# Moving SBUF-by-SBUF products from POOL to DVE in the first part of a mixing stage, with the rotary tables scaled later and a key's high part written twice by ACT

## The chip, the cores and the metric

The kernel runs on one core of one Trainium2 chip. The metric is device time in microseconds (us) of one execution. Five engines work side by side, each on its own queue in order: PE (matrix products), DVE (VectorE), ACT (ScalarE), POOL (GpSimd) and SP, which here only issues DMAs. They wait for each other by semaphores.

## The reference

Two encoder layers over a sequence of 512 tokens of width 1024, all in float32. Each layer does

    x += 0.5 * swiglu_1(rms_norm(x))
    z  = rms_norm(x) @ W_in                 # columns for four mixers of four heads each
    A: 2-D neighbourhood attention with a learned bias      (nq, nk, nv)
    B: sliding window attention, rotary, sink logit          (sq, sk, sv)
    C: three dilated windows merged, rotary                  (dq, dk, dv)
    D: latent attention with a decoupled rotary key          (cq, ckv, kpe)
    x += concat(rms_norm of each mixer's output) @ W_out
    x += 0.5 * swiglu_2(rms_norm(x))
    x += sigmoid(rms_norm(x) @ W_gate) * (p @ W_proj)

and a last rms_norm follows. `rope` turns the halves of a vector: (x1 cos - x2 sin, x2 cos + x1 sin). In mixer A a bias is added to each score and everything outside a window is masked.

## The kernel before

Activations lie transposed: 128 partitions of the width, 512 tokens along the row. Every float32 operand of a large product is split in two, a high part rounded to the matrix unit's format and a low part that is the rest, and a product is three matmuls (high by high, high by low, low by high; `mm3y`, L200, one step of three matmuls at a time). Weights are split as they arrive: `pieces` (L155) loads 512 KB into `raw`, ACT writes the high part `wh` (L178), and L179 and L180 subtract it to give the low part `wl`. This subtraction is on POOL while `self.mixing` is true and on DVE otherwise. `raw` has two buffers, `wh` and `wl` three each.

The mixing stage (`mix`, L680) runs once per layer. First it projects nq0 and nk0; behind them the norm's factor `rb` is spread over the partitions (L715) and multiplied in by DVE (`plain`, L358). Then 16 heads run in order, four of each mixer, as a software pipeline: scores of head n (`qk`), transposed probabilities (`tr`) and their product with the values (`pv`) of the head before, and between them steps of the projections still to come (`pump`, with `STEPS` per head). The heads of mixer A are n = 0 to 3.

Tiles that the change touches:

- A key is kept as `t`, whose two halves hold its high part twice, and `klz`, which holds the low part of one head's 64 rows and zeros elsewhere (`stack`, L338, with `scale` None). ACT writes the high part (L344), DVE copies it to the other 64 partitions (L345) and subtracts (L349). It runs for nk0, nk1, sk, dk0 and dk1.
- `rope` (L326): ACT swaps the halves into `sw`, DVE multiplies the projection by `cos`, POOL multiplies `sw` by `sin` (L334), DVE adds.
- L719 and L720 multiply the two rotary tables `cos` and `sin` (names `tab`) by `rb` on POOL, before the first head.
- For each head of mixer A a bias of 128x896 is loaded into `nb` by a DMA from POOL's queue (L649) and subtracted from the mask by POOL (L651). `nb` has one buffer, so the load of a head waits until DVE has read the bias of the head before (L410).
- The scores go to one of four PSUM buffers `s`. L410 adds the mask on DVE, takes the row minimum and so frees the buffer.
- `value` (L363): DVE multiplies a projected value by `rb` (L367), PE transposes it some steps later (L374).

PE's and SP's instructions are issued as the code is written. On DVE, ACT and POOL a scheduler sets the order when the program is built; on the chip each engine keeps that order.

Of the kernel before, what the change touches and what calls it, by code (L numbers as in the profile page):

```python
# [9 lines left out]
F32 = mybir.dt.float32  # L10
F32R = mybir.dt.float32r
AF = mybir.ActivationFunctionType
ALU = mybir.AluOpType
# [21 lines left out]
class Encoder:  # L35
# [119 lines left out]
    def pieces(self):  # L155
        nc, a = self.nc, self.a
        first = True
        for src, cuts in self.plan():
            n = cuts[-1][0] + cuts[-1][1] * cuts[-1][2]
            raw = self.tile("raw", [128, 1024], F32, 2)  # L160
            src = src.rearrange("p k m -> p (k m)") if len(src.shape) == 3 else src
            if first:
                nc.sync.dma_start(raw[:, :512], src[:, :512])
                nc.sync.dma_start(self.x[0], a["x"][:, 0])
                nc.sync.dma_start(self.x[1], a["x"][:, 1])
                nc.sync.dma_start(self.x[2], a["x"][:, 2])
                nc.sync.dma_start(raw[:, 512:], src[:, 512:])
                for k in range(3, KC):
                    nc.sync.dma_start(self.x[k], a["x"][:, k])
                first = False  # L170
            else:
                nc.sync.dma_start(raw[:, :n], src)
            for o, k, m in cuts:
                c = k * m
                hi = self.tile("wh", [128, 512], F32R, 3)[:, :c]
                lo = self.tile("wl", [128, 512], F32R, 3)[:, :c]
                r = raw[:, o:o + c]
                nc.scalar.activation(hi, r, AF.Copy)  # L178
                eng = nc.gpsimd if self.mixing else nc.vector  # L179
                eng.tensor_tensor(out=lo, in0=r, in1=hi.bitcast(F32), op=ALU.subtract)  # L180
                yield (hi.rearrange("p (k m) -> p k m", k=k), lo.rearrange("p (k m) -> p k m", k=k))

    def take(self):
        if not self.ready:
# [141 lines left out]
    def rope(self, p, scale=None):  # L326
        nc = self.nc
        sw = self.tmp()
        for b in range(4):
            o = b ^ 1  # L330
            nc.scalar.activation(sw[32 * b:32 * b + 32], p[32 * o:32 * o + 32], AF.Copy)  # L331
        u = self.tmp()
        nc.vector.tensor_tensor(u, p, self.cosr, op=ALU.mult)
        nc.gpsimd.tensor_tensor(out=sw, in0=sw, in1=self.sinr, op=ALU.mult)  # L334
        nc.vector.tensor_tensor(out=u, in0=u, in1=sw, op=ALU.add)
        return self.stack(u, scale)

    def stack(self, u, scale):  # L338
        nc = self.nc
        t = self.big()  # L340
        lo, up = slice(0, 64), slice(64, 128)
        if scale is None:
            for e, r, w in ((0, lo, up), (1, up, lo)):
                nc.scalar.activation(t[r, e], u[r], AF.Copy)  # L344
                nc.vector.tensor_copy(t[w, e], t[r, e].bitcast(F32))  # L345
            kl = self.klz[self.nkl % 2]
            self.nkl += 1
            for e, r in ((0, lo), (1, up)):
                nc.vector.tensor_tensor(out=kl[r, e], in0=u[r], in1=t[r, e].bitcast(F32), op=ALU.subtract)  # L349
            return t, kl  # L350
        for e, r in ((0, lo), (1, up)):
            nc.scalar.activation(t[r, e], u[r], AF.Copy, scale=scale)
        for e, r, w in ((0, lo, up), (1, up, lo)):
            nc.vector.scalar_tensor_tensor(out=t[w, e], in0=u[r], scalar=scale, in1=t[r, e].bitcast(F32),
                                           op0=ALU.mult, op1=ALU.subtract)
        return t
# [154 lines left out]
        self.t[key] = self.plain(self.p, scale)  # L511

    def d_rope(self, key, i, scale=None):
        yield from self.proj(i)
        self.t[key] = self.rope(self.p, scale)

# [123 lines left out]
    def heads(self, l):  # L640
        nc, a = self.nc, self.a
        S = lambda e: slice(64 * e, 64 * e + 64)
        off, wid = (0, 256, 256, 640), (256, 384, 384, 256)
        base = dict(band=True, sink=None, perm=False)

        def na(h):
            j, e = divmod(h, 2)
            nb = self.tile("nb", [128, 896], F32, 1)
            self.tc.keep_in_program_order(nc.gpsimd.dma_start(nb, a["na_bias"][l, h]))  # L649
            v = nb.rearrange("p (b r w) -> p b r w", b=7, r=8)  # L650
            nc.gpsimd.tensor_tensor(out=v, in0=self.na_mask.unsqueeze(2).to_broadcast([128, 7, 8, 16]),  # L651
                                    in1=v, op=ALU.subtract)
            return dict(base, q=self.t[f"nq{j}"], k=self.t[f"nk{j}"], v=self.t[f"nv{j}"], rows=S(e), odd=e,
                        perm=True, mask=lambda t: nb[:, off[t]:off[t] + wid[t]])

        def swa(i):
            j, e = divmod(i, 2)
            h = 2 * e + j
            return dict(base, q=self.t[f"sq{j}"], k=self.t["sk"], v=self.t["sv"], rows=S(e), odd=e,
                        mask=lambda t: self.swa_mask[:, (128 if t == 0 else 0):(256 if t == 3 else 384)],  # L660
                        sink=(self.nsink[:, l, h:h + 1], self.sink[:, l, h:h + 1]))

        def dil(h):
            j, e = divmod(h, 2)
            return dict(base, q=self.t[f"dq{j}"], k=self.t[f"dk{j}"], v=self.t[f"dv{j}"], rows=S(e), odd=e,
                        band=False, mask=lambda t: self.dil_mask[:, 384 - 128 * t:896 - 128 * t])

        def mla(h):
            j, e = divmod(h, 2)
            return dict(base, q=self.t[f"mq{h}"], k=self.t[f"mk{h}"], v=self.t[f"mv{j}"], rows=None,  # L670
                        odd=e, band=False, mask=None)

        out = []
        for f, gi, keys in ((na, 0, ("nq{0}", "nk{0}", "nv{0}")), (swa, 1, ("sk", "sq{0}", "sv")),
                            (mla, 2, ("mv{0}",)), (dil, 3, ("dv{0}",))):
            for h in range(4):
                out.append((f, gi, h, [k.format(h // 2) for k in keys]))
        return out

    def mix(self, l, nxt):  # L680
        nc, a = self.nc, self.a
# [6 lines left out]
        cos = self.tile("tab", [128, T], F32, 2)  # L688
        sin = self.tile("tab", [128, T], F32, 2)
# [26 lines left out]
        self.t["nq0"] = self.plain(p0, s)  # L716
        self.t["nk0"] = self.plain(p1)
        self.done |= {"nq0", "nk0"}
        nc.gpsimd.tensor_tensor(out=cos, in0=cos, in1=self.rb, op=ALU.mult)  # L719
        nc.gpsimd.tensor_tensor(out=sin, in0=sin, in1=self.rb, op=ALU.mult)  # L720

        self.mixing = True
        last, prev, pend, rg = None, None, None, None
        todo = self.heads(l)
        self.need(*todo[0][3])
# [2 lines left out]
        for n, item in enumerate(todo + [None]):  # L728
            h = None
            if item is not None:  # L730
                f, gi, i, keys = item
                self.need(*keys)
                h = f(i)
                if h["odd"]:
                    h["y"], h["l8"] = mate["y"], mate["l8"]
                else:
                    h["y"], h["l8"] = self.ytile(), self.tile("l8", [128, 2, 4], F32, 2)
                    mate = h
                h["end"] = gi if i == 3 else None
            if n == 9:  # L740
                self.stream += [(f"part{i}", self.d_part(i)) for i in range(4)]
            for b in range(6):
                if b == 0 and last is not None:
                    self.pv(last, 3)
                    if last["odd"]:
                        self.pair_end(last)
                        pend = last["end"]
                if h is not None and b < 4:
                    self.qk(h, b)
                if prev is not None:  # L750
                    if 3 <= b:
                        self.pv(prev, b - 3)
                    if 1 <= b < 5:
                        self.tr(prev, b - 1)
                quota += STEPS[n] / 6.0
                self.pump(int(quota))
                quota -= int(quota)
                if b == 3 and pend is not None:
                    rg = self.rstat(self.gacc, 256)
                if b == 5 and rg is not None:  # L760
                    self.group_end(l, pend, rg)
                    pend, rg = None, None
            last, prev = prev, h
# [24 lines left out]
        for m in range(4):  # L788
            if m % 2 == 0:
                w = self.take()  # L790
# [195 lines left out]
```

## Time and profile before

| | us |
|---|---|
| median of 3 timed runs | 2148.17 (2146.65 to 2148.85) |
| the profiled execution | 2144.82 |
| its span in the trace | 2143.0 |

The profiled execution is 3.35 us below the median of the timed runs, and 1.82 us of it lie outside the span.

| engine | busy us | share of the span |
|---|---|---|
| PE | 2091.5 | 98% |
| DVE | 1210.1 | 56% |
| ACT | 929.2 | 43% |
| POOL | 283.3 | 13% |

PE is busy nearly all the time; what it does not do is found by asking for its waits and then by looking at those places in the order of time. A busy share over the whole span says little about the mixing stages, which are two stretches of about 260 us each, from about 380 us and from about 1437 us.

### The profile page before, as it was taken

How to read it: one execution, taken by the hardware profiler on the slowest of the kernel's cores; microseconds unless marked ns; L12 is line 12 of the kernel's file. 1: busy time of each engine (PE TensorE's matmuls, PEld its weight loads, DVE VectorE, ACT ScalarE, POOL GpSimd, SP SyncE). 2: the span in 40 equal slices, each digit the busy share in tenths (PEclk: the TensorE clock that was granted, in tenths of full speed). 3: DMA queues.
4: the chain of work that ended last, by engine and by line, in shares of the span. 5: the costliest groups of instructions: out<-in, count | busy, mean ns of one | idle time of the engine just before them, and what ended most of it. 6: DMA issues, size and time to landing. Idle time of an engine off the chain costs nothing.

```text
span 2143.0 us, 25740 instructions
## 1 busy us (share of the span) xinstructions
PE 2091.5 (98%) x9564; PEld 1726.3 (81%) x9564; DVE 1210.1 (56%) x1926; ACT 929.2 (43%) x1690; POOL 283.3 (13%) x234
## 2 busy tenths in 40 slices
PE   8999999899999999999999999998999999999997
PEld 6888888777788888888888888886878888888886
DVE  5444445567776444455654444556787744444554
ACT  4332333477754322333433233335777533233343
POOL 2000001444321000001100000025432200000011
PEclk9999999999999999999999999999999999999998
DMA  3233223213112223232322232232221222232322
GB/s 130 98 109 101 98 86 111 95 58 84 40 60 99 99 87 101 97 105 92 100 98 99 93 104 94 89 113 94 64 60 50 69 99 98 85 106 95 107 90 89
DMA packets 63357, 195.37 MB, mean 91 GB/s; under 512 B 7552, under 2 KB 15872, under 8 KB 63232
## 3 DMA queue, kind: packets, MB, share of 16 engines
q1 hardware_dynamic: 61808, 187.92, 26.5%
q0 software_dynamic: 1280, 5.77, 1.0%
q8 instruction: 75, 1.23, 0.2%
q14 instruction: 50, 0.41, 0.1%
q10 hardware_dynamic: 144, 0.05, 0.0%
HBM read 189.51 MB, written 2.10 MB: 89 GB/s over the span
## 4 chain that ended last, share of the span: by engine, by line
PE 91%; DVE 5%; ACT 2%; issue 1%; DMA 1%; POOL 0%; SPq 0%; POOLq 0%; DVEq 0%; ACTq 0%
PE ps L205 15%; PE ps L206 15%; PE ps L207 15%; PE s L207 13%; PE s L205 13%; PE s L206 13%; PE pv L461 2%; PE s L445 2%; PE s L403 1%; DVE klz L349 1%; PE s L404 1%; ACT tmp L331 1%; PE s L230 1%; DVE PT L449 1%; ACT PT L448 0%
## 5 line engine op out<-in xcount | busy, mean ns | idle before, releaser
L178 ACT ACTIVATE wh<-raw 128x512 fp32r<-128x512 f32 (+1 forms) x712 | 437.7, 615 | 959.4 <-PE ps L206 440.7
L180 DVE TENSOR_TENSOR wl<-raw,wh 128x512 fp32r<-128x512 f32 (+1 forms) x614 | 435.4, 709 | 405.8 <-ACT wh L178 399.4
L205 PE MATMUL ps<-act,wh 128*128 128x512 f32 x616 | 248.5, 403 | 5.9 <-ACT act L127 5.9
L221 POOL TENSOR_TENSOR acc<-acc,tmp 128x512 f32<-128x512 f32 x54 | 72.1, 1336 | 1362.8 <-ACT tmp L220 1362.6
L205 PE MATMUL ps<-big,wh 128*128 128x512 f32 x616 | 246.3, 400 | 0.0
L206 PE MATMUL ps<-act,wh 128*128 128x512 f32 x616 | 244.2, 396 | 1.8 <-DVE act L128 1.7
L207 PE MATMUL ps<-act,wl 128*128 128x512 f32 x616 | 243.1, 395 | 0.0
L207 PE MATMUL ps<-big,wl 128*128 128x512 f32 x616 | 241.0, 391 | 0.0
L206 PE MATMUL ps<-big,wh 128*128 128x512 f32 x616 | 241.0, 391 | 0.0
L205 PE MATMUL s<-big,wh 128*128 128x512 f32 x520 | 202.4, 389 | 0.0
L205 PE MATMUL s<-act,wh 128*128 128x512 f32 x520 | 202.4, 389 | 0.0
L207 PE MATMUL s<-act,wl 128*128 128x512 f32 x520 | 202.3, 389 | 0.0
L206 PE MATMUL s<-act,wh 128*128 128x512 f32 x520 | 202.3, 389 | 0.0
L207 PE MATMUL s<-big,wl 128*128 128x512 f32 x520 | 202.3, 389 | 0.0
L206 PE MATMUL s<-big,wh 128*128 128x512 f32 x520 | 202.3, 389 | 0.0
L180 POOL TENSOR_TENSOR wl<-raw,wh 128x512 fp32r<-128x512 f32 (+1 forms) x98 | 128.0, 1306 | 265.2 <-ACT wh L178 259.5
L205 PEld LDWEIGHTS ps<-act,wh 128*128 128x128 f32 x616 | 117.5, 191 | 27.6 <-ACT act L127 6.0
L206 PEld LDWEIGHTS ps<-act,wh 128*128 128x128 f32 x616 | 117.4, 191 | 27.4 <-DVE act L128 6.0
L207 PEld LDWEIGHTS ps<-act,wl 128*128 128x128 f32 x616 | 117.5, 191 | 24.7
L207 PEld LDWEIGHTS ps<-big,wl 128*128 128x128 f32 x616 | 116.2, 189 | 24.9
L206 PEld LDWEIGHTS ps<-big,wh 128*128 128x128 f32 x616 | 116.5, 189 | 21.6
L205 PEld LDWEIGHTS ps<-big,wh 128*128 128x128 f32 x616 | 116.3, 189 | 21.3
(174 smaller groups left out, 3377.6 us busy)
## 6 DMA issues: line engine op xcount, KB each, us to landing
raw<-in_ffn_gu SPq DMA_DIRECT2D x175, 512.0 KB, 3.5
raw<-in_ffn_d SPq DMA_DIRECT2D x64, 512.0 KB, 3.5
raw<-in_w_in SPq DMA_DIRECT2D x40, 512.0 KB, 3.5
raw<-in_ffn_d SPq DMA_DIRECT2D x64, 192.0 KB, 2.5
raw<-in_w_out SPq DMA_DIRECT2D x16, 512.0 KB, 3.5
raw<-in_ple SPq DMA_DIRECT2D x16, 384.0 KB, 3.1
raw<-in_ple SPq DMA_DIRECT2D x16, 256.0 KB, 2.6
nb<-in_na_bias POOLq DMA_DIRECT2D x8, 448.0 KB, 3.6
```

The source lines that it names most:

```text
L178: nc.scalar.activation(hi, r, AF.Copy)
L180: eng.tensor_tensor(out=lo, in0=r, in1=hi.bitcast(F32), op=ALU.subtract)
L205: nc.tensor.matmul(ps, lhsT=wh[:, k], rhs=x[:, 0], start=start and k == 0, stop=False)
L206: nc.tensor.matmul(ps, lhsT=wh[:, k], rhs=x[:, 1], start=False, stop=False)
L207: nc.tensor.matmul(ps, lhsT=wl[:, k], rhs=x[:, 0], start=False, stop=stop and k == last)
L221: eng.tensor_tensor(out=acc, in0=acc, in1=sq, op=ALU.add)
L230: nc.tensor.matmul(ss[:, t:t + 1], lhsT=acc[:, t * 128:(t + 1) * 128], rhs=self.ones, start=True, stop=True)
L331: nc.scalar.activation(sw[32 * b:32 * b + 32], p[32 * o:32 * o + 32], AF.Copy)
L349: nc.vector.tensor_tensor(out=kl[r, e], in0=u[r], in1=t[r, e].bitcast(F32), op=ALU.subtract)
L403: nc.tensor.matmul(s, lhsT=q[:, e, qs], rhs=k[0][:, e, k0:k1], start=True, stop=False)
L445: nc.tensor.transpose(tp[:, t * 128:(t + 1) * 128], h["P"][t][:, o:o + 128], self.ident)
L461: nc.tensor.matmul(pv[:, c], lhsT=vb, rhs=h["pt"][b][:, i, c], start=b == 0 and i == 0, stop=b == 3 and i == 1, skip_group_check=True)
```

## The change

The part of the weights, tables, masks and rotary products that the first heads need moves from POOL to DVE. `mixing` becomes true when head 3 begins and not before head 0, so that the low parts of the weights taken until then are made by DVE, as is the rotary product of `sk` (the new `side`). The subtraction of the bias from the mask is on DVE for all heads of mixer A. The tables are scaled by DVE when the projection of `sk` is started in the code. In `stack`, ACT writes the high part of a key to both places and DVE copies nothing.

```diff
@@ pieces
                 nc.scalar.activation(hi, r, AF.Copy)
-                eng = nc.gpsimd if self.mixing else nc.vector
+                eng = self.side()
                 eng.tensor_tensor(out=lo, in0=r, in1=hi.bitcast(F32), op=ALU.subtract)
...
+    def side(self):
+        return self.nc.gpsimd if self.mixing else self.nc.vector
@@ rope
         nc.vector.tensor_tensor(u, p, self.cosr, op=ALU.mult)
-        nc.gpsimd.tensor_tensor(out=sw, in0=sw, in1=self.sinr, op=ALU.mult)
+        self.side().tensor_tensor(out=sw, in0=sw, in1=self.sinr, op=ALU.mult)
@@ stack
                 nc.scalar.activation(t[r, e], u[r], AF.Copy)
-                nc.vector.tensor_copy(t[w, e], t[r, e].bitcast(F32))
+                nc.scalar.activation(t[w, e], u[r], AF.Copy)
@@ d_rope
+        if key == "sk":
+            for t in (self.cosr, self.sinr):
+                self.nc.vector.tensor_tensor(out=t, in0=t, in1=self.rb, op=ALU.mult)
@@ heads, na
-            nc.gpsimd.tensor_tensor(out=v, in0=self.na_mask.unsqueeze(2).to_broadcast([128, 7, 8, 16]),
+            nc.vector.tensor_tensor(out=v, in0=self.na_mask.unsqueeze(2).to_broadcast([128, 7, 8, 16]),
@@ mix
-        nc.gpsimd.tensor_tensor(out=cos, in0=cos, in1=self.rb, op=ALU.mult)
-        nc.gpsimd.tensor_tensor(out=sin, in0=sin, in1=self.rb, op=ALU.mult)
-
-        self.mixing = True
...
+            if n == 3:
+                self.mixing = True
```

In the new file the lines from `take` to `d_rope` have numbers higher by 3, and those from `d_lat` to the head loop by 6. The order of PE's rows is the same in both programs. In each layer, 12 subtractions for `wl`, 4 for `nb`, 2 for `tab` and 1 rotary product go from POOL to DVE, and 10 copies from DVE to ACT.

The first place is on DVE, at the beginning of the first mixing stage, from the first use of `rb` to the value product of nv0 (L367 before, L370 now). Before:

```order
L360 TENSOR_TENSOR tmp_2905<-ps_2820,rb_2903 128x8x4x16
L360 TENSOR_TENSOR tmp_2912<-ps_2855,rb_2903 128x8x4x16
L354 SCALAR_TENSOR_TENSOR big_2907<-tmp_2905,big_2907 64x512 x2
L345 CAST big_2914<-big_2914 64x512
L349 TENSOR_TENSOR klz_1043<-tmp_2912,big_2914 64x512
L345 CAST big_2914<-big_2914 64x512
L349 TENSOR_TENSOR klz_1043<-tmp_2912,big_2914 64x512
L367 TENSOR_TENSOR tmp_2958<-ps_2923,rb_2903 128x8x4x16
```

And now:

```order
L363 TENSOR_TENSOR tmp_2905<-ps_2820,rb_2903 128x8x4x16
L363 TENSOR_TENSOR tmp_2912<-ps_2855,rb_2903 128x8x4x16
L519 TENSOR_TENSOR tab_2816<-tab_2816,rb_2903 128x512
L519 TENSOR_TENSOR tab_2817<-tab_2817,rb_2903 128x512
L657 TENSOR_TENSOR nb_2983<-na_mask,nb_2983 128x896
L357 SCALAR_TENSOR_TENSOR big_2907<-tmp_2905,big_2907 64x512 x2
L352 TENSOR_TENSOR klz_1043<-tmp_2912,big_2914 64x512 x2
L370 TENSOR_TENSOR tmp_2956<-ps_2921,rb_2903 128x8x4x16
```

The two copies are gone from between, and the scaling of both tables and the mask of head 0 stand ahead of the value product.

The second place is on DVE too, at the scores of head 1 (L410 before, L413 now; `klz_1044` belongs to nk1). Before:

```order
L360 TENSOR_TENSOR tmp_3097<-ps_3034,rb_2903 128x8x4x16
L449 TENSOR_TENSOR PT_3094<-s_3091,PT_3094 128x256
L345 CAST big_3099<-big_3099 64x512
L349 TENSOR_TENSOR klz_1044<-tmp_3097,big_3099 64x512
L345 CAST big_3099<-big_3099 64x512
L349 TENSOR_TENSOR klz_1044<-tmp_3097,big_3099 64x512
L410 ISA P_3076,ne_3072<-s_3073,nb_3069 128x256
```

And now:

```order
L180 TENSOR_TENSOR wl_3106<-raw_3055,wh_3105 128x512
L657 TENSOR_TENSOR nb_3067<-na_mask,nb_3067 128x896
L363 TENSOR_TENSOR tmp_3095<-ps_3032,rb_2903 128x8x4x16
L413 ISA P_3074,ne_3070<-s_3071,nb_3067 128x256
L413 ISA ne_3070 128x1
L413 ISA P_3086,ne_3070<-s_3083,nb_3067 128x384
L413 ISA ne_3070 128x1
L180 TENSOR_TENSOR wl_3157<-raw_3154,wh_3156 128x512
L452 TENSOR_TENSOR PT_3092<-s_3089,PT_3092 128x256
L352 TENSOR_TENSOR klz_1044<-tmp_3095,big_3097 64x512
```

The first two blocks of head 1 now stand ahead of the key's low parts, and behind the mask product, which waits for the bias's DMA.

The third place is on ACT, at the same point of the program, between the first transposed probabilities (L448 before, L451 now) and the exponentials of head 1 (L416 before, L419 now). Before:

```order
L448 ACTIVATE PT_3094<-s_3091 128x256
L344 ACTIVATE big_3099<-tmp_3097 64x512 x2
L448 ACTIVATE PT_3127<-s_3123 128x384
L178 ACTIVATE wh_3187<-raw_3156 128x512
L416 ACTIVATE P_3076,l_2989<-P_3076,ne_3072 128x256
```

And now:

```order
L451 ACTIVATE PT_3092<-s_3089 128x256
L347 ACTIVATE big_3097<-tmp_3095 64x512
L348 ACTIVATE big_3097<-tmp_3095 64x512
L347 ACTIVATE big_3097<-tmp_3095 64x512
L348 ACTIVATE big_3097<-tmp_3095 64x512
L419 ACTIVATE P_3074,l_2987<-P_3074,ne_3070 128x256
L419 ACTIVATE P_3086,l_2987<-P_3086,ne_3070 128x384
L451 ACTIVATE PT_3125<-s_3121 128x384
```

Two more writes stand ahead of the exponentials, and the second block of transposed probabilities is now behind two exponentials.

## Rows read from the trace of the kernel before

**Rows 1.** Waits of the whole span: total us, times, longest.

```profile
PE s L403 <- DVE ne L410: 10.7, 4, 3.4
```

**Rows 2.** PE in order of time: start, us, [idle before, who ended it].

```profile
397.61 1.11 PE L374 MATMUL s<-ident,tmp 128*128 128x128 f32 x4 [3.05 <-DVE tmp L367]
417.25 0.38 PE L403 MATMUL s<-big,big 128*128 128x256 f32 x1 [2.99 <-DVE ne L410]
444.72 0.44 PE L403 MATMUL s<-big,big 128*128 128x384 f32 x1 [2.15 <-DVE ne L410]
468.24 0.39 PE L461 MATMUL pv<-PT,big 128*128 128x256 f32 x1 [0.68 <-DVE PT L449]
...
1454.02 0.66 PE L374 MATMUL s<-ident,tmp 128*128 128x128 f32 x4 [2.91 <-DVE tmp L367]
1472.47 0.39 PE L403 MATMUL s<-act,act 128*128 128x256 f32 x1 [3.40 <-DVE ne L410]
1499.95 0.53 PE L403 MATMUL s<-act,act 128*128 128x384 f32 x1 [2.17 <-DVE ne L410]
```

**Rows 3.** Stretches behind those waits: length, PE busy, granted clock, DMA.

```profile
398.00:402.00 4.00, 4.00 (x16) 0.62 0.00 0
418.00:422.00 4.00, 4.00 (x15) 0.57 0.52 188
445.00:449.00 4.00, 4.00 (x15) 0.57 0.00 0
1455.00:1460.00 5.00, 5.00 (x26) 1.00 0.31 103
1473.00:1478.00 5.00, 5.00 (x20) 0.67 0.44 149
1500.00:1505.00 5.00, 5.00 (x21) 0.66 0.00 2
```

**Rows 4.** DVE in order of time, up to the first wait's end.

```profile
387.72 1.29 DVE L360 TENSOR_TENSOR tmp<-ps,rb 128x512 f32<-128x512 f32 x2 [3.79 <-ACT rb L248]
...
393.38 2.31 DVE L349 TENSOR_TENSOR klz<-tmp,big 64x512 fp32r<-64x512 f32 x1
395.70 0.42 DVE L345 CAST big<-big 64x512 fp32r<-64x512 f32 x1
396.14 0.69 DVE L349 TENSOR_TENSOR klz<-tmp,big 64x512 fp32r<-64x512 f32 x1
396.86 0.69 DVE L367 TENSOR_TENSOR tmp<-ps,rb 128x512 f32<-128x512 f32 x1
```

**Rows 5.** Groups by line and shape, DVE and ACT: count, busy us, mean ns.

```profile
L180 DVE TENSOR_TENSOR wl<-raw,wh 128x512 fp32r<-128x512 f32 x4 | 2.8, 688 | 3.0 <-ACT wh L178 3.0
...
L410 DVE CUSTOM_DVE_ANT_0 P<-s,nb 128x384 f32<-128x384 f32 x8 | 4.3, 553 | 0.8 <-PE s L404 0.8
...
L344 ACT ACTIVATE big<-tmp 64x512 fp32r<-64x512 f32 x6 | 3.8, 628 | 0.9 <-DVE tmp L335 0.8
```

**Rows 6.** Instructions on the bias tile: duration min/median/max in ns.

```profile
L651 POOL TENSOR_TENSOR nb<-na_mask,nb x8: 2097/2132/2308, 401.6 to 1493.7; 128x896 f32<-128x896 f32 x8
...
DMA to landing us min/median/max: 3.2/3.6/5.0
```

**Rows 7.** DVE in order of time, heads 0 to 3 of the first layer.

```profile
406.21 0.42 DVE L410 CUSTOM_DVE_ANT_0 P<-s,nb 128x256 f32<-128x256 f32 x1
...
410.26 0.69 DVE L360 TENSOR_TENSOR tmp<-ps,rb 128x512 f32<-128x512 f32 x1 [2.19 <-PE ps L207]
...
416.76 0.42 DVE L410 CUSTOM_DVE_ANT_0 P<-s,nb 128x256 f32<-128x256 f32 x1
...
438.81 2.51 DVE L349 TENSOR_TENSOR klz<-tmp,big 64x512 fp32r<-64x512 f32 x1
```

**Rows 8.** First part of each mixing stage: length; busy of PE, PEld, DVE, ACT, POOL; clock.

```profile
380.00:450.00 70.00, 61.66 (x289) 50.88 (x289) 42.34 (x77) 38.87 (x84) 38.15 (x28) 0.93 0.25 87
1437.00:1505.00 68.00, 59.37 (x287) 49.21 (x287) 42.38 (x77) 38.20 (x84) 38.19 (x28) 0.95 0.27 90
```

## The prediction

> **What bounds the kernel now.** I read the waits of PE first, since PE is the busiest engine. The largest group is PE waiting for DVE's masking line before it can write scores [rows 1]. PE in order of time shows where: three waits at the start of each mixing stage, at the same program points in both layers [rows 2]. The first (call it S1) ends with the value product of nv0, 3.05 and 2.91 us. The second (S2) ends with the masking of head 1's first block, 2.99 and 3.40 us. The third (S3) ends with that of head 3, 2.15 and 2.17 us. Together they are 16.67 us. Then I asked for the granted clock behind each [rows 3]: in five of six places it averages 0.57 to 0.67, between the levels of 1.2 and 2.4 GHz, though PE is busy the whole stretch; behind the 2.91 us wait it stays at 1.00. A stretch of length L at a mean clock c loses (1 - c) L: 1.52, 1.72, 1.72, 0, 1.65 and 1.70, together 8.31 us. So the three places cost 16.67 + 8.31 = 24.98 us.
>
> Why is DVE late there? The reader compares two rows with the same operation and shape [rows 4]: the low part of a key takes 2.31 us at 393.38 and 0.69 us at 396.14. In the stretch around them POOL is busy 38.15 of 70 us, with operands in SBUF as this one has [rows 8]. The value product, which reads PSUM, takes its 0.69 us. So I read the long ones as DVE held up by POOL on SBUF operands. The 9.83 us from 387.72 to the end of the value product at 397.55 hold S1. At S2 the stack of nk1 stands between 410.26 + 0.69 and the first masking at 416.76 [rows 7]. S3 is the same with sk, whose first low part takes 2.51 us.
>
> **The change part by part.** Without POOL's products until head 3, I take DVE's instructions at their short durations: 0.69 us for 64x512 or 128x512 [rows 4, 5].
>
> S1. The new order on DVE is two products with rb (1.29 us, as before), two tables (2 x 0.69), the mask of head 0, two and two operations on 64x512 (4 x 0.69) and the value product (0.69). The mask on DVE, 128x896, is not in the trace. From below it is 0.69 us (128x512), from above POOL's own 2.13 us [rows 5, 6]. 553 ns at 384 columns and 688 ns at 512 give 1.05 ns a column, so I take 0.69 + 384 x 1.05 ns = 1.09 us, being nearest to rows of the same engine. The sum is 7.21 us, so the value product ends at 394.93; PE arrives at 397.61 - 3.05 = 394.56 and starts some 0.06 us behind it. S1 shrinks to 0.4 us in either layer. The mask's upper bound would make it 1.5. The mask also waits for the bias's DMA, which now has nothing ahead of it on POOL but the small operation that rb itself needs. That is at least a transpose and a copy before 387.72, so it is issued by about 386.5 and lands by 390.1 at the median of 3.6 us, by 391.5 at 5.0 us. DVE reaches the mask at 387.72 + 1.29 + 1.38 = 390.39. Bounds: 0 to 1.1 us more; I take 0. A rest of 0.4 us should not lower the clock: the wait of 0.68 us at 468.24 [rows 2] is too short by every case in the rows, where the lowered clock follows waits of 2.15 us and more.
>
> S2. PE asked for a buffer at 417.25 - 2.99 = 414.26. Now the mask of head 1, the product for nk1 and the first masking come in that order, ahead of the low parts. The DMA of the bias starts when head 0's last block is masked, at 406.21 + 0.42 = 406.63 if nothing were earlier; with 3.2 to 5.0 us, 1.09, 0.69 and 0.42 us the buffer is free between 412.0 and 413.8 on the old time scale. That is before 414.26, so S2 goes, with a margin of 0.4 to 2.2 us. As all the heads' work moves with PE, what is late next is the bias's DMA, and behind its waiting mask product on DVE stand nk1's product and head 1's maskings.
>
> S3. PE asked at 444.72 - 2.15 = 442.57. Taking the old begin of the first low part, 438.81, although a copy goes from ahead of it, the mask (1.09), one low part (0.69) and the masking (0.42) end at 441.0. S3 goes, with 1.5 us to spare for a hold-up by POOL, which has its subtractions again from head 3 on; the long row shows 2.51 - 0.69 = 1.8 us of it, so at the worst 0.3 us of S3 stays.
>
> Weights. 12 subtractions of 0.69 us per layer come to DVE, 8.3 us. In the stretch DVE idles 70 - 42.34 = 27.7 us [rows 8], and each is made well ahead of its matmuls, as three buffers allow. I take 0 and keep it as a rival.
>
> The key's copies. Three of five stacks per layer lie in this stretch: six copies go from DVE, and ACT gets six writes of 0.63 us [rows 5], 3.8 us on 38.87 of 70. At S2's place ACT's exponentials and the second transposed block come 1.26 us later. On the path this is between 0 and 1.26 us for each of the six stacks of both layers, 0 to 7.6; the blocks are wanted about when they come, so I take 0.2 each, nearest the lower end, 1.3 us. The other two stacks (dk0, dk1) lie far behind, where no scores of the next head queue behind them; I cost them at nothing, and without that cover they are at most 4 x 1.26 = 5 us.
>
> The copy on DVE takes 0.42 us when it is not held up [rows 4], ACT's write 0.63. The Trainium skill (VectorE: DVE Perf Modes, Mode 2×_2P) says why the copy is the cheap kind there: with one source, both in SBUF, the engine streams it over two ports and gives two results a cycle, which a product of two tensors cannot have. The trace agrees: 0.42 us against 0.69 for the same columns. By that rule the copies should have stayed on DVE once POOL is quiet; kept there, they would add 2 x 0.42 us to S1's sum in each layer, 1.7 us in all, against my 1.3 us on ACT. So by rule and row this part of the change is worth next to nothing.
>
> Sum: 24.98 - 2 x 0.4 - 1.3 = 22.9 us. The profiled execution of 2144.82 becomes 2121.9. It was 3.35 us under the median of the timed runs; on their scale the forecast is 2125.3 us.
>
> **The rivals.** First, ACT takes over as the late engine. For it: its work rises to 42.7 us in a stretch that shrinks from 70 to about 58 us, 74%, and its queue has both key writes and exponentials. Against it: the margin is 26%, and none of the seven waits shown ends with ACT [rows 2]. At the upper bound, 7.6 us, with a lowered clock behind two of the six at 1.7 us, the gain is 22.9 - 6.3 - 3.4 = 13.2: about 2135 us.
>
> Second, on the other side, DVE paces the stretch. It gains 12 x 0.69 + 4 x 1.09 + 3 x 0.69 = 14.7 us of work and loses six copies of 0.42, 2.5 us. If its 27.7 us of waiting stay, because each block still comes when PE and the DMA of a single bias buffer give it, the stretch is 12.2 us longer in each layer: 2148.2 + 24.4, about 2173 us. It decides once less than 12.2 of the 27.7 us can be filled. Against it: a good part of that idle time is DVE waiting for projections that come late because PE was stalled, and the hold-ups, 1.6 us in one row alone, are not in this sum.
>
> Third, the long durations are not POOL's doing but come from the key's layout, 64 partitions read and written. Then S1 stays as it is, and S2 and S3 go only by the new order: waits of 10.71 us, clock of 6.79 us, less 1.3 on ACT, 16.2 us in all, so 2132. The row of 0.69 us with the same layout speaks against it.
>
> Fourth, another wait of the same size follows at once in each place, for the bias or for weights: 2148 us.
>
> **How the numbers follow.** Forecast 0.66, by its own terms 2118 to 2132 (all 24.98 and a few us of small waits behind them, or the upper bounds of mask, DMA and half of ACT's). ACT (2135) and the layout (2132) 0.18 together. Nothing gained 0.07. DVE as the pace, 0.09. 0.2% is about what a measurement of this kernel can tell, 4.3 us. Faster is 0.66 + 0.18 = 0.84, same 0.07, slower 0.09. The range 2117 to 2140 holds the first two cases but for their tails, 0.8.
>
> **What would show it.** Right: PE's waits at the first value transposes under 1 us; none at head 1's and head 3's scores; granted clock near 1.00 in the first part of both stages; the low parts of keys at 0.69 us; the new mask on DVE near 1.1 us and not waiting over 1 us for its DMA. Wrong: PE waiting for transposed probabilities or for an exponential of ACT in heads 0 to 2, or for a low part of a weight from DVE; low parts of keys still above 1 us while POOL is idle; a mask product that blocks DVE for several us.

## The result and the profile after

The changed kernel takes 2122.69 us (median of four runs, 2119.75 to 2123.83) against 2147.41 us for the kernel before in the same session: ratio 0.9884, 95% interval 0.9868 to 0.9899. It is 24.7 us faster; the forecast was 2125.3, with a range of 2117 to 2140. On a second chip it took 2123.21 us, ratio 0.9895 (0.9881 to 0.9910).

The profiled execution took 2119.75 us, its span 2117.9; the forecast on that scale was 2121.9. Of the 25.1 us that the span lost, 10.8 are busy time of PE (2091.5 to 2080.7 us with the same 9564 matmuls, while the mean granted clock rose from 0.991 to 0.996) and 14.3 are idle time.

The waits of PE over the whole span of the changed kernel (total, times, longest):

```profile
PE ps L208 <- ACT act L127: 5.9, 1, 5.9
PE s L233 <- DVE acc L224: 4.4, 1, 4.4
PE pv L464 <- DVE PT L452: 4.3, 13, 0.7
PE s L377 <- DVE tmp L372: 4.0, 2, 2.0
...
PE s L377 <- DVE tmp L370: 0.7, 2, 0.4
```

The line that led before, scores behind DVE's masking [rows 1], is not in the list any more. The last row is what S1's waits became. PE in order of time shows both places (idle before, and who ended it, in brackets):

```profile
395.18 0.66 PE L377 MATMUL s<-ident,tmp 128*128 128x128 f32 x4 [0.30 <-DVE tmp L370]
496.52 0.66 PE L377 MATMUL s<-ident,tmp 128*128 128x128 f32 x4 [2.01 <-DVE tmp L372]
1438.58 0.66 PE L377 MATMUL s<-ident,tmp 128*128 128x128 f32 x4 [0.44 <-DVE tmp L370]
1539.85 0.66 PE L377 MATMUL s<-ident,tmp 128*128 128x128 f32 x4 [2.01 <-DVE tmp L372]
```

S1 has shrunk from 3.05 and 2.91 us [rows 2] to 0.30 and 0.44; S2 and S3 have no row. The two rows of 2.01 us (call the place S4, the value product of mv0) belong to no part of the change: before has them too, 3.9 us in all.

The granted clock is the number behind POOL's busy time, in stretches of the changed kernel (length; busy of PE, PEld, DVE, ACT, POOL; clock; DMA share; GB/s). The first two are the first parts of the mixing stages [rows 8], the last two lie around S4:

```profile
381.00:440.00 59.00, 58.23 (x298) 48.86 (x298) 44.33 (x92) 41.83 (x92) 9.15 (x9) 1.00 0.31 102
1424.00:1482.00 58.00, 57.09 (x293) 47.88 (x292) 43.52 (x89) 40.74 (x88) 7.92 (x9) 1.00 0.32 105
496.00:502.00 6.00, 4.95 (x18) 3.86 (x19) 4.24 (x8) 3.01 (x6) 0.95 (x1) 0.72 0.30 45
1539.00:1546.00 7.00, 5.36 (x27) 4.33 (x28) 5.46 (x10) 4.28 (x9) 1.79 (x1) 1.00 0.32 48
```

Before, PE worked 61.66 us in 70 at a clock of 0.93; now 58.23 in 59 at 1.00. POOL fell from 38 us to 8 or 9. S4 in layer 2 kept its clock; before, two stretches there lost some:

```profile
1560.00:1566.00 6.00, 3.35 (x16) 2.37 (x15) 4.98 (x8) 2.69 (x6) 1.81 (x2) 0.92 0.81 176
1566.00:1572.00 6.00, 6.00 (x25) 4.83 (x24) 4.82 (x8) 4.14 (x10) 2.06 (x2) 0.80 0.12 31
```

That is at most 0.08 x 6 + 0.20 x 6 = 1.7 us (PE was not busy all through the first of them), which this one execution gained at a place that the change doesn't touch.

DVE of the changed kernel in order of time, up to the value product that S1 waits for, and two masks: that of head 1, which waited for its DMA, and that of head 3, the longest:

```profile
388.04 1.29 DVE L363 TENSOR_TENSOR tmp<-ps,rb 128x512 f32<-128x512 f32 x2
389.24 1.29 DVE L519 TENSOR_TENSOR tab<-tab,rb 128x512 f32<-128x512 f32 x2
390.44 1.08 DVE L657 TENSOR_TENSOR nb<-na_mask,nb 128x896 f32<-128x896 f32 x1
391.56 1.40 DVE L357 SCALAR_TENSOR_TENSOR big<-tmp,big 64x512 fp32r<-64x512 f32 x2
393.00 1.41 DVE L352 TENSOR_TENSOR klz<-tmp,big 64x512 fp32r<-64x512 f32 x2
394.43 0.69 DVE L370 TENSOR_TENSOR tmp<-ps,rb 128x512 f32<-128x512 f32 x1
...
405.67 1.09 DVE L657 TENSOR_TENSOR nb<-na_mask,nb 128x896 f32<-128x896 f32 x1 [1.22 <-DMA nb<-in_na_bias]
...
428.45 2.19 DVE L657 TENSOR_TENSOR nb<-na_mask,nb 128x896 f32<-128x896 f32 x1
```

From 388.04 to 395.12 the chain is 7.08 us, though three operations have come to it and only two casts have left it; before it was 9.83 [rows 4]. And the same groups over the whole span (duration min/median/max in ns):

```profile
L352 DVE TENSOR_TENSOR klz<-tmp,big x10: 673/686/690, 393.0 to 577.6; 64x512 fp32r<-64x512 f32 x10
L352 DVE TENSOR_TENSOR klz<-tmp,act x10: 673/686/691, 1436.4 to 1620.7; 64x512 fp32r<-64x512 f32 x10
```

All 20 low parts of keys take 0.67 to 0.69 us; before, the same groups reached 2514 and 2518 ns:

```profile
L349 DVE TENSOR_TENSOR klz<-tmp,big x10: 682/1173/2514, 393.4 to 591.2; 64x512 fp32r<-64x512 f32 x10
L349 DVE TENSOR_TENSOR klz<-tmp,act x10: 682/690/2518, 1449.9 to 1646.0; 64x512 fp32r<-64x512 f32 x10
```

### The profile page after: what moved, and what is told of

It is laid out like the page before. It is cut to its first block, busy times and chain, and to the rows that moved or that the text cites. A ratio compares the mean times of both kernels' runs of the same rounds, so it can differ in the third digit from the quotient of the medians.

```text
span 2117.9 us, 25721 instructions
## 1 busy us (share of the span) xinstructions
PE 2080.7 (98%) x9564; PEld 1718.0 (81%) x9564; DVE 1211.0 (57%) x1944; ACT 942.5 (45%) x1710; POOL 225.5 (11%) x196
## 4 chain that ended last, share of the span: by engine, by line
PE 92%; DVE 3%; ACT 2%; issue 1%; DMA 1%; POOL 0%; POOLq 0%; SPq 0%; DVEq 0%; ACTq 0%
PE ps L208 15%; PE ps L209 15%; PE ps L210 15%; PE s L210 13%; PE s L209 13%; PE s L208 13%; PE pv L464 2%; PE s L448 2%; ACT tmp L334 1%; PE s L406 1%; PE s L407 1%; PE s L233 1%; DVE PT L452 1%; PE s L244 0%; DVE tmp L338 0%
## 5 line engine op out<-in xcount | busy, mean ns | idle before, releaser
L180 DVE TENSOR_TENSOR wl<-raw,wh 128x512 fp32r<-128x512 f32 (+1 forms) x638 | 452.4, 710 | 415.6 <-ACT wh L178 411.9
L210 PEld LDWEIGHTS ps<-big,wl 128*128 128x128 f32 x616 | 115.6, 188 | 24.7
L285 DVE TENSOR_TENSOR tmp<-tmp,s 128x512 f32<-128x512 f32 x88 | 60.5, 688 | 127.5 <-PE s L210 127.5
```

What stands on the lines that cost most here:

```text
L210: nc.tensor.matmul(ps, lhsT=wl[:, k], rhs=x[:, 0], start=False, stop=stop and k == last)
L285: nc.vector.tensor_tensor(gr, gr, up, op=ALU.mult)
```

## Experiments

The theory, called H where the expectations name it: POOL's operations on SBUF operands hold DVE's up, and the time comes from taking POOL's away. The rivals are named in the expectations by what they say: the copies' place in DVE's chain, the weights, DVE becoming the pace. The experiments ran on several chips. The kernel before ran beside each group, with medians between 2145.18 and 2147.41 us, so a difference of 2 us between two variants says nothing.

**The copies alone.** The kernel before, with one line of the change:

```diff
-                nc.vector.tensor_copy(t[w, e], t[r, e].bitcast(F32))
+                nc.scalar.activation(t[w, e], u[r], AF.Copy)
```

> The kernel before with one edit alone: ACT writes the key's high part twice. Theory H (POOL's operations on SBUF operands hold DVE's up): the low parts of keys stay above 1 us on the mean, the first wait S1 shrinks from 3.0 by the two copies of its chain, 1.8 us, to about 1.2 us; S2 and S3 shrink by more, since two or three held-up copies leave each of their stacks. About 2 x (1.8 + 2.5 + 2.1) = 13 us of waits and a part of the lowered clock: 2130 to 2136 us. Rival C (the copies are the cause, whatever POOL does): all of the gain, 2121 to 2125 us. Rival N (the copies are worth nothing, as the forecast said of this part): 2145 to 2149 us.

2124.08 us against 2145.66, ratio 0.9901 (0.9886 to 0.9916): 21.6 us, nearly the whole gain, with POOL as busy as before (283.3 us in both profiles). H's number was missed and rival C's came. DVE of this kernel at S1, and at head 1 (S2):

```profile
389.03 2.82 DVE L354 SCALAR_TENSOR_TENSOR big<-tmp,big 64x512 fp32r<-64x512 f32 x2
391.88 1.41 DVE L349 TENSOR_TENSOR klz<-tmp,big 64x512 fp32r<-64x512 f32 x2
393.32 0.69 DVE L367 TENSOR_TENSOR tmp<-ps,rb 128x512 f32<-128x512 f32 x1
...
406.82 0.68 DVE L349 TENSOR_TENSOR klz<-tmp,big 64x512 fp32r<-64x512 f32 x1
409.87 0.42 DVE L410 CUSTOM_DVE_ANT_0 P<-s,nb 128x256 f32<-128x256 f32 x1 [2.36 <-POOL nb L651]
```

The pair at 389.03 is still held up (2.82 us for what takes 1.40 above). But the two low parts run at once, in 1.41 us, and the value product begins at 393.32 where it began at 396.86 [rows 4]. Counted from the first product, at 387.64 here and 387.72 before, that is 3.46 us earlier, more than S1's wait. Two things have changed there: the casts are gone from DVE's chain, and POOL's next weight subtraction comes later, since ScalarE makes the weight's high part behind its extra writes. Before, and here:

```profile
391.77 1.31 POOL L180 TENSOR_TENSOR wl<-raw,wh 128x512 fp32r<-128x512 f32 x1 [0.39 <-ACT wh L178]
```

```profile
393.01 1.43 POOL L180 TENSOR_TENSOR wl<-raw,wh 128x512 fp32r<-128x512 f32 x1 [1.70 <-ACT wh L178]
```

At S2 the masking now stands between the two low parts and waits 2.36 us for POOL's mask, and a rest of PE's wait is left:

```profile
410.35 0.39 PE L403 MATMUL s<-big,big 128*128 128x256 f32 x1 [1.05 <-DVE ne L410]
```

**All but the copies.** The changed kernel with the line above turned back:

> The changed kernel with the copy of the key's high part back on DVE. Theory H and the forecast's working: POOL is quiet, so a copy takes 0.42 us; S1 grows by 0.84 us in each layer from 0.3 or 0.4, and the rest stays hidden: 2122.7 + 1.7 = 2124.4 us (2123 to 2126). Rival C (the copies are the cause): at least half of the gain is lost, 2134 us or more.

2127.71 us, ratio 0.9919 (0.9905 to 0.9934): some 5 us over the changed kernel, not 1.7, between H's number and the rival's. Its copies all take 0.42 us, but S1 has 1.73 us. Beside the two copies a weight subtraction now stands ahead of the value product, which the forecast's 2 x 0.42 us did not count:

```profile
395.70 0.69 DVE L180 TENSOR_TENSOR wl<-raw,wh 128x512 fp32r<-128x512 f32 x1
```

```profile
397.05 0.66 PE L377 MATMUL s<-ident,tmp 128*128 128x128 f32 x4 [1.73 <-DVE tmp L370]
```

Over both layers S1 is 3.4 us in place of 0.7, and 1.6 us come at the scores of another head: 4.3 of the 5. Rival C, that the copies are the cause whatever POOL does, is refuted: it wanted 2134 us or more. So either half of the change alone brings 18 to 22 us and both bring 22 to 25. They take away the same waits, and don't add.

**Does a later POOL do it?** ScalarE's extra writes also make the weights' parts come later on POOL. This run has that without relieving DVE: the kernel before plus

```diff
                 nc.scalar.activation(t[r, e], u[r], AF.Copy)
+                nc.scalar.activation(self.tile("scr", [128, 512], mybir.dt.bfloat16, 1)[w], u[r], AF.Copy)
                 nc.vector.tensor_copy(t[w, e], t[r, e].bitcast(F32))
```

> The kernel before, in which ScalarE, at each of the places where the change has it write a copy of k's high part, writes as many elements into a scratch tile that nothing reads (64x512, bfloat16); VectorE still makes the copies. The copies on ScalarE alone gave 21.6 us. They do two things: they take two casts out of VectorE's chain ahead of klz, and they hold ScalarE up so that POOL gets its next weight 1.24 us later (wl at 393.01 in place of 391.77). This kernel has the second without the first. Theory (it is VectorE's own chain that counts: two casts and what holds them up): no gain, 2143 to 2150 us, the S1 wait 2 to 3 us. Rival (it is the meeting in time with POOL's wl that counts): klz runs free, at 0.7 us, and most of the gain comes without the casts being gone, 2124 to 2135 us.

2141.11 us against 2145.18, ratio 0.9978 (0.9968 to 0.9988), between the two expected ranges and nearer the theory's. DVE at S1, POOL's subtraction there, then PE at S1 and S2:

```profile
393.45 0.42 DVE L346 CAST big<-big 64x512 fp32r<-64x512 f32 x1
393.89 0.68 DVE L350 TENSOR_TENSOR klz<-tmp,big 64x512 fp32r<-64x512 f32 x1
394.58 1.42 DVE L346 CAST big<-big 64x512 fp32r<-64x512 f32 x1
396.02 2.30 DVE L350 TENSOR_TENSOR klz<-tmp,big 64x512 fp32r<-64x512 f32 x1
```

```profile
393.94 1.78 POOL L180 TENSOR_TENSOR wl<-raw,wh 128x512 fp32r<-128x512 f32 x1 [1.05 <-ACT wh L178]
```

```profile
399.09 0.66 PE L375 MATMUL s<-ident,tmp 128*128 128x128 f32 x4 [3.02 <-DVE tmp L368]
416.85 0.39 PE L404 MATMUL s<-big,big 128*128 128x256 f32 x1 [1.17 <-DVE ne L411]
```

S1 is as before, and so is S3 (2.18 us). POOL's subtraction came later, 4.71 us behind DVE's first product of the stage (4.05 before, 5.37 with the copies alone), but with the casts in its chain DVE was no further by then: the second cast and low part met POOL's work. Only S2 fell, from 2.99 and 3.40 to 1.17 and 1.11 us, since the longer ScalarE queue led the scheduler to put the second cast and low part behind the masking. So a later POOL alone, here by 0.66 us, does not remove S1 or S3. If the order at S2 is worth the 4 us of this run in the kernel with the copies alone too, the other 17 of the 21.6 come with the casts' going; that is an estimate by difference. Whether the casts' going would do without the later POOL was not run: with the copies alone the low parts ran 4.24 to 5.65 us behind the first product, and a subtraction at the old 4.05 would have met them.

**The weights back on POOL** from the start of the stage; mask, tables, sine product and copies as in the change. The switch of the weights is set before head 0 again, that of the sine product stays:

```diff
+        self.mixing = True
         last, prev, pend, rg = None, None, None, None
...
-            if n == 3:
-                self.mixing = True
```

> The changed kernel with the 12 subtractions for the weights' low parts back on POOL from head 0 on; masks, tables and the product for sk stay on DVE. Theory H: POOL is busy 16 us more in the first part and DVE's low parts of keys, tables and masks are held up again (means above 1 us); S1 comes back with 1 to 2 us in each layer and S2 or S3 in part: 2128 to 2138 us. Rival W (the gain is work and order on DVE, not a hold-up): 8.3 us less work on DVE per layer, so not slower than the changed kernel, 2120 to 2123 us.

2129.39 us, ratio 0.9927 (0.9912 to 0.9942): 6 to 7 us are lost, H's number, but not at H's places. S1 has no wait, the low parts of keys stay at 0.69 us. The scheduler put the mask of head 0 behind S1's value product here, at 400.5. The time turns up elsewhere, at the transposed probabilities:

```profile
PE s L448 <- DVE PT L452: 4.4, 3, 2.2
```

That group is not in the changed kernel. DVE's masks reach 1962 ns here and wait 10.4 us for the bias's DMA (2.7 in the changed kernel), whose first issue on POOL stands at 395.7, behind the subtractions, and at 385.6 there. So part of what the weights on POOL cost is the queue in front of that DMA and not a hold-up; how much was not separated.

**POOL busy on purpose.** The changed kernel, in which POOL makes each of the stage's first 12 subtractions twice more, over 384 of the 512 columns, into a scratch tile; `repeat` is true from before head 0 until head 3:

```diff
                 eng.tensor_tensor(out=lo, in0=r, in1=hi.bitcast(F32), op=ALU.subtract)
+                if self.repeat:
+                    for _ in range(2):
+                        scr = self.tile("scr", [128, 384], F32, 1)
+                        nc.gpsimd.tensor_tensor(out=scr, in0=r[:, 0:384], in1=hi[:, 0:384].bitcast(F32), op=ALU.subtract)
```

> The changed kernel, and POOL makes each of the first 12 weight subtractions of a mixing stage twice more, over 384 columns, into a scratch tile that nothing reads. DVE's work is that of the changed kernel. Theory H: about 24 operations of 1 us on POOL in each first part hold DVE's SBUF products up as before; the low parts of keys and of weights take over 1 us on the mean, two or three of the waits of PE come back: 2130 to 2142 us. Rival W (work and order): 2122 to 2125 us.

2137.14 us, ratio 0.9961 (0.9946 to 0.9975): 14 us lost to work that nothing reads, and H's number. Over the whole span DVE is busy 1224.2 us with the same 1944 instructions for which it takes 1211.0 in the changed kernel. In the first part POOL is busy 35.47 us of 59, DVE's mask rises to a median of 1515 ns from 1093, and S2 is back in the first layer:

```profile
381.00:440.00 59.00, 53.65 (x263) 44.17 (x262) 44.58 (x77) 34.59 (x73) 35.47 (x30) 0.97 0.31 102
```

```profile
416.05 0.39 PE L411 MATMUL s<-big,big 128*128 128x256 f32 x1 [3.10 <-DVE ne L418]
```

Not all of the 14 us is hold-up. The first bias DMA is issued at 396.9, behind POOL's added work, and DVE waits 7.9 us for these DMAs (2.7 in the changed kernel); and the scheduler put the low parts of nk1 ahead of the masking at S2 again, 2.08 us. S1 has no wait, and of the 20 low parts of keys the longest took 1372 ns, with a median of 687.

**The mask back on POOL:**

```diff
-            nc.vector.tensor_tensor(out=v, in0=self.na_mask...
+            nc.gpsimd.tensor_tensor(out=v, in0=self.na_mask...
```

> The changed kernel with the subtraction of the bias from the mask back on POOL (2.1 us each, four per layer). Forecast's working: DVE loses 1.09 us per head and no longer stands waiting for the bias's DMA, S1 shrinks from 0.3 or 0.4 us to 0; the four operations on POOL hold up at most two or three DVE products by 1 us each: 2120 to 2125 us, no difference from the changed kernel. Rival (the second rival's place: the mask product on DVE behind a single bias buffer is the tight spot): 2117 to 2120 us. Rival H in full (any POOL operation in this stretch brings waits back): 2127 us or more.

2128.65 us, ratio 0.9923 (0.9908 to 0.9937); my 2120 to 2125 was missed and H's number met. POOL's mask and the DVE pair beside it, and what S1 makes of it:

```profile
390.03 2.33 POOL L657 TENSOR_TENSOR nb<-na_mask,nb 128x896 f32<-128x896 f32 x1 [3.77 <-DMA nb<-in_na_bias]
```

```profile
390.41 3.22 DVE L357 SCALAR_TENSOR_TENSOR big<-tmp,big 64x512 fp32r<-64x512 f32 x2
```

```profile
395.85 0.66 PE L377 MATMUL s<-ident,tmp 128*128 128x128 f32 x4 [1.12 <-DVE tmp L370]
```

1.82 us more on the pair, where the mask on DVE costs 1.08. PE further waits 2.6 us for ScalarE's transposed probabilities, and at the transposition L448 1.2 and 1.1 us for DVE, two groups that the profile of the changed kernel doesn't have.

**Copies and weights only.** The kernel before with ScalarE's copies and the weights on DVE until head 3; mask, tables and sine product stay on POOL.

> The kernel before with two parts of the change: ScalarE writes both copies of k's high part, and the weights' low parts are made by VectorE before head 3. The mask (L651), the table products and sk's sine product stay on POOL. The copies alone gave 2124.1 us, the whole change 2122.7. Theory (with the copies on ScalarE, what POOL still holds up is small, and the weights are most of it): 2121 to 2125 us, the S1 wait 0 to 0.5 us. Rival (the mask and the tables on POOL hold VectorE up ahead of S1, as where the mask alone was put back): 2126 to 2130 us, S1 wait about 1 us.

2126.65 us, ratio 0.9912 (0.9897 to 0.9927): no better than the copies alone. The subtractions on DVE now meet POOL's mask, which runs from 394.83 to 397.14:

```profile
394.49 3.20 DVE L180 TENSOR_TENSOR wl<-raw,wh 128x512 fp32r<-128x512 f32 x2
```

Moving some products to DVE while others stay on POOL puts more under the hold-up. The rival's number came, but not by its place: S1 has no wait. Nor do the waits explain the number: PE is idle 40.5 us here and 41.5 with the copies alone, and its busy time is 2083.5 against 2080.9 us.

**More on DVE, or longer.** Three variants of the changed kernel: no weight subtraction and no rotary product of the stage on POOL (the switch left out); these on DVE in heads 6 to 8 as well; the switch at head 5 in place of 3.

> The changed kernel with all weight subtractions and rotary products of the mixing stage on DVE, none on POOL. Theory H alone: no hold-ups anywhere, the 2.0 us wait at the value of mv0 shrinks, 2115 to 2121 us. Rival D (the price of DVE's work, the forecast's second rival): 37 subtractions and 6 rotary products more per layer, about 30 us on an engine that already works 142 us in the rest of the stage, so blocks come late in heads 4 to 15: 2128 to 2150 us.

> The changed kernel with the weight subtractions on DVE in heads 6 to 8 as well, where the wait of 2.0 us for the value of mv0 stands in both layers. Theory H: the operations ahead of that value (two of 1.77 us together in the trace of before) run at 0.69 us each, the wait shrinks by 0.5 to 2 us and with it a lowered clock worth 0 to 1.7 us in each layer: 2117 to 2121 us. Rival D: three or four subtractions of 0.69 us more stand ahead of the value: the wait grows to 3 or 4 us, 2124 to 2130 us.

> The changed kernel with the switch back to POOL when head 5 begins instead of head 3: about 8 subtractions and one or two rotary products more per layer on DVE. Theory H: the mask of head 3, 2.19 us in one trace, and the short waits of 0.2 to 0.7 us for transposed probabilities shrink; 2120 to 2123 us. Rival D: 6 to 7 us more work on DVE in two heads, waits for transposed probabilities grow: 2124 to 2130 us.

In this order: 2124.86 us, ratio 0.9904 (0.9889 to 0.9919); 2125.75, 0.9908 (0.9892 to 0.9925); and 2121.89, 0.9890 (0.9876 to 0.9905). None can be told from the change for certain. The first missed both expected numbers; the second met the rival's, without its longer wait; the third met H's, and the mask of head 3 did fall to 1.08 us. S4 stays at 2.0 to 2.1 us in all three. In the first POOL computes nothing in the last 9 us before S4's value product and DVE's products there take 0.69 us or less, so S4 is no hold-up by POOL. DVE doesn't become the pace even with everything.

**S4 by another order.** The switch at head 5, and the transposes of mv0's value three steps later, `self.later.append([6 if key == "mv0" else 3, finish, key])`. The changed kernel ran beside it.

> The changed kernel with the switch at head 5 in place of 3, and the transposes of mv0's value put off: TensorE does three more projection steps ahead of them. What it is for: the largest wait that the changed kernel has left is TensorE's 2.0 us per layer at L377 for VectorE's tmp (L372), and the clock was 0.72 behind it in layer 1. Theory (the wait is only a question of order, VectorE catches up when TensorE has other work): both waits go, 2 x 2.0 us and 0 to 3 us of lowered clock, 2115 to 2119 us. Rival (VectorE is behind by its backlog and the wait turns up at the next consumer, or the step put ahead needs a PSUM buffer that isn't free): 2120 to 2126 us with a wait of 1 to 2 us on another line.

> The changed kernel once more, on the same chip as the two others: 2121 to 2125 us. It shows how far the two others' times can be set against it; below 2120 or above 2126 us the differences of 1 to 3 us between the variants say nothing.

2122.46 us, ratio 0.9894 (0.9878 to 0.9911), against 2123.21 for the changed kernel (the 0.9895 given at the start): the rival's number, and its sign, a wait on another line. DVE is late at that point also when PE has other work first:

```profile
496.71 0.47 PE L208 MATMUL ps<-keep,wh 128*128 128x512 f32 x1 [1.36 <-DVE tmp L372]
498.40 0.51 PE L208 MATMUL ps<-keep,wh 128*128 128x512 f32 x1 [0.77 <-DVE tmp L589]
```

2.13 us in place of 2.01, and PE's wait for ScalarE's exponentials at L448 grows from 1.4 to 3.8 us. No version measured here is faster than the change by more than the noise.

## Why the prediction was right, and where it was not

**Right: the places and the total.** S1, S2, S3 and their clock were 24.98 us; with rests of 0.8 and 1.3 for ScalarE, 22.9 us were to go. The span lost 25.1. Idle time fell by 14.3 us, forecast 16.67 - 0.8 - 1.3 = 14.6. The clock's 8.31 came as 10.8, of which up to 1.7 at S4 in layer 2 are not the change's. But the total says little for the reason given: the copies alone bring 2124.1 us, as near to the forecast of 2125.3 as the whole change. It came out right because the forecast counted the waits that would go, and they go in more than one way; in that it was lucky.

**Right: the terms of S1.** The chain was put at 7.21 us and took 7.08, the mask at 1.09 and took 1.08, the rest of S1 at 0.4 and was 0.30 and 0.44. No clock was lost behind it. The mask of head 0 did not wait for its DMA.

**Right: S2, S3, and DVE's room.** S2 went although head 1's mask did wait 1.22 us for its DMA, inside the margin of 0.4 to 2.2. At S3 the mask was held up by a subtraction of POOL's (2.19 us, above), 1.1 over its own duration, inside the margin of 1.5. The 12 subtractions per layer cost no wait that the list shows: DVE is busy 43.52 of 58 us in layer 2 and PE doesn't wait for a weight.

**Wrong: the key's copies.** The step that failed is "by rule and row this part of the change is worth next to nothing". Alone it brings 21.6 us, and undoing it costs 5, not 1.7. The Trainium skill (VectorE: DVE Perf Modes, Mode 2×_2P) was used for why DVE's copy is short. The trace agrees, 0.42 us against 0.69 for a product of two tensors, and it decided nothing. The casts of the kernel before, the first at S1 and the others with their low parts at S2, show why:

```profile
391.94 1.42 DVE L345 CAST big<-big 64x512 fp32r<-64x512 f32 x1
...
411.76 1.17 DVE L345 CAST big<-big 64x512 fp32r<-64x512 f32 x1
412.94 1.68 DVE L349 TENSOR_TENSOR klz<-tmp,big 64x512 fp32r<-64x512 f32 x1
414.64 0.42 DVE L345 CAST big<-big 64x512 fp32r<-64x512 f32 x1
415.07 1.66 DVE L349 TENSOR_TENSOR klz<-tmp,big 64x512 fp32r<-64x512 f32 x1
```

The casts are held up too, to 1.42 and 1.17 us here; I had priced them at the short duration, in a stage where POOL was already quiet. And they stand in the chain that PE waits for, each pushing a low part towards POOL's next subtraction. At S1 they and what they pushed are 3.46 us, more than the whole wait of 3.05. I had given all of it to POOL's operations, because the change moved those as well.

**Not shown when I wrote it: that a product reading PSUM is not held up.** I took this from the value product at 396.86, but POOL computed nothing between 395.14 and 400.37, so that row says nothing. The run with the copies alone shows it: the value product takes 0.69 us from 393.32, inside POOL's subtraction of 393.01 to 394.44.

**What H is worth.** That POOL holds DVE up is shown by adding POOL work alone (13.2 us more of DVE's busy time for the same instructions) and by the mask (3.22 against 1.40 us for one pair). Taking POOL's products away without the copies brings 18 us. But it is one of two ways to the same waits, each enough for most of the gain: with the copies off DVE, all the other parts together are worth 0.6 to 3.1 us, by 21.6 against 22.2 to 24.7, which these runs can hardly tell from nothing.

**Not seen: ScalarE's cost.** I charged 0.2 us for each of six stacks, 1.3 us in all (six times 0.2 is 1.2). With ScalarE writing as much for nothing the kernel was 4 us faster, and the waits at S2 were 4.1 us shorter, by the order that followed. In the changed kernel the added writes took 0.63 us each, all 20, and PE's wait for ScalarE's exponentials at L448 is 1.4 us as before.

**The rivals.** ScalarE late (2135): in the profiled execution no wait of the first part ends with it, and in the second profile of the same kernel two of 0.46 us do. DVE as the pace (2173): refuted, above all by the variant without the switch. The key's layout as the cause of long low parts (2132): refuted by 20 of 20 at 0.69 us. Its price was wrong too: it let S1 stand, though two casts leave S1's chain. The same waits following (2148): none did.

Open is why the mask alone, back on POOL, costs 6 us when S1's share of it is 1.5. The 2.6 us behind ScalarE and the 1.2 and 1.1 behind DVE at L448 make up the rest in the list of waits; why those waits come with the mask was not followed.

## What to carry to other kernels

Price each part of a change alone, in the kernel before, at the durations that its instructions have there, held up or not; where two parts shorten the same chain, their gains need not add (here 21.6 and 18 us alone, 22 to 25 together). When an engine is late by 2 to 3 us at a few places, try first to take a short instruction out of the chain before the wait, even if the engine that gets it is slower at it: here one changed line brought 21.6 us. And when work is put back on a queue to test a hold-up, look at what else waits in that queue and at how the scheduler's order changed.

## What the runs showed of the chip

A wait of PE of about 2 us does not settle the clock behind it: in the changed kernel the two rows of 2.01 us at S4 were followed by 0.72 in layer 1 and 1.00 in layer 2, and behind 1.17 us at S2 in the run with idle ScalarE writes it stayed at 1.00. A cast on DVE, 0.42 us alone, took up to 1.58 us in the kernel before, where POOL worked beside it; ScalarE's write of the same elements took 630 to 634 ns at all 20 places.
